# Gate/up weights of a SwiGLU layer: two of the four block sums made by accumulating loads

## Chip, cores and metric

The kernel runs on one core of a Trainium2 chip. The metric is the device time of one execution in microseconds, as the median of several runs. The core's engines are named as the profile names them: PE (TensorE matmuls, with PEld for its weight loads), DVE (VectorE), ACT (ScalarE), POOL (GpSimd) and SP (SyncE, which issues most transfers). Transfers run on 16 DMA engines.

## What is computed

One encoder layer for 512 tokens of width 2048: a combined projection, sliding-window attention and gated linear attention side by side, an output projection, and a SwiGLU feed-forward block of width 5632, with RMS norms between. The part that matters here is the feed-forward block:

```python
h = rmsnorm(x, ffn_norm_w[l])
x = x + (jax.nn.silu(h @ w_gate[l]) * (h @ w_up[l])) @ w_down[l]
```

`w_gate` and `w_up` are 2048 x 5632, `w_down` is 5632 x 2048, all float32.

## The kernel before

Every float32 operand of a matmul is split into a high part (rounded to the PE's fp32r) and a low part (the remainder), and each product is made of three matmuls: high x high, high x low, low x high. The splits are a copy on ACT (high) and a subtraction on DVE (low).

The order of all instructions is written out by hand in the program: each engine executes its own list in order and waits for others by semaphores. Buffers are kept in lists of free slots. The large buffers ("b" in the profile, 16 slots of 128 partitions x 4 KB, `s4` in the code) are handed out in the order in which they came free; a slot can be handed out in the program's order before its last reader has finished on the chip, and the instruction that fills it then waits.

The gate and up projections are run by the class `Feed`. There are 22 column blocks of 256 for each of the two weights, hence 44 units (gate and up alternate), and each unit has four pieces, 176 in all. A piece is a weight block of 512 rows x 256 columns (512 KB). It is handled as two halves, each a 2 x 2 arrangement of 128 x 128 blocks, and multiplied by Strassen's method in Winograd's form: for each half there are seven products in place of eight, each with three matmuls, so a piece has 42 matmuls of 128 x 128 by 128 x 256. This needs, for each half, the raw blocks 11, 12, 21, 22 (three of them as operands of products) and four sums of blocks:

- Z0 = block 12 + block 11, and Z1 = block 21 + block 11 (one DVE instruction, L1095, in which block 11 is broadcast),
- Z2 = Z0 + block 21 (L1096),
- Z3 = Z2 + block 22 (L1097).

The steps of a piece, with their lines:

- `load` (L1073 to L1082): SP issues one transfer of the whole piece into a slot `r`, in rows of 1 KB. Up to three loaded pieces are held ahead of their split.
- `sums` (L1084 to L1097): takes a second slot `S` and has DVE make the four sums.
- `split` (L1099 to L1116): ACT copies the three raw blocks (128x768) and the four sums (128x1024) to two high slots, L1107; DVE makes two low slots, L1112. Then `r` and `S` are given back, and `load` is called again.
- `products` (L1118 to L1141): the 42 matmuls on PE, lines L1137 to L1139, after which the four slots are given back.

`run` (L1183 to L1201) goes through the pieces. For piece i it calls `load`, then `sums` of piece i+2, then `split` of piece i+1, then `products` of piece i, and then one step of pending work, which is mostly `evac`: at the end of a unit, ACT and DVE take the sums out of PSUM (L1153 to L1162) and `finish` scales them and applies SiLU (gate) or multiplies by the gate and stores 512 KB to DRAM from SP (up, L1178 to L1181). The first loads of the stage are issued in the last job of the output projection (`before_out`, L1029). In the last unit `down_start` begins to load for the down projection; its step for piece 3 has POOL reload 16 tiles of the residual (L1244).

Apart from these reloads and 16 residual loads (L954) and 16 stores (L1011) before the stage, POOL has almost nothing to do.

Of the kernel before, what the change touches and what calls it, by code (L numbers as in the profile page):

```python
# [15 lines left out]
F32 = mybir.dt.float32  # L16
# [3 lines left out]
OP = mybir.AluOpType  # L20
# [3 lines left out]
P = 128  # L24
D = 2048
S = 512
KT = D // P
# [28 lines left out]
def _constants():  # L56
# [7 lines left out]
    masks = np.stack([j[:, None] <= j[None, :], j[:, None] >= j[None, :]]).astype(np.uint32)  # L64
    resets = np.ones((2, S), np.float32)
    resets[0, 0::P] = 0.0
# [45 lines left out]
def put(*slots):  # L112
    for s in slots:
        if s.home is not None:
            s.home.free.append(s.i)


def layer(nc, tc, x, attn_norm_w, w_in, rel_table, gw_f, gb_f, gw_b, gb_b, gla_norm_w, w_out,
# [3 lines left out]
    w_gate, w_up, w_down, out = w_gate[0], w_up[0], w_down[0], out[0]  # L122
    pe, act, dve, pool, sp = nc.tensor, nc.scalar, nc.vector, nc.gpsimd, nc.sync
    mm = pe.matmul

    with tc.manual_schedule(), \
# [6 lines left out]
        s4 = Slots(p4, N4, 1024, "b")  # L133
# [73 lines left out]
        def piece512(w, col, kt):  # L207

            ws = w if isinstance(w, list) else [(w, col)]
            n = 512 // len(ws)  # L210
            segs = []
            for i, (wi, c) in enumerate(ws):
                src = wi[kt * P:(kt + 2) * P, c:c + n].rearrange("(k p) c -> p k c", p=P)
                segs.append((src, lambda t, i=i, n=n: t.rearrange("p (k c) -> p k c", k=2)[:, :, i * n:(i + 1) * n]))
            return segs
# [36 lines left out]
        def job(kind, pieces, kts, acts, evac, rate=0.0, before=None, start=None, limit=None):  # L252

            j = Job()
            j.kind, j.kts, j.acts, j.evac, j.rate, j.before, j.start, j.limit = \
                kind, kts, acts, evac, rate, before, start, limit
            j.first = len(st.halves)
            st.add(pieces)
            j.n = len(st.halves) - j.first
            jobs.append(j)  # L260
            return j
# [347 lines left out]
        def gla_operands():  # L609
# [4 lines left out]
            for d, w in enumerate((gw_f[0], gw_b[0])):  # L614
                pool.memset(G["gw"][d].t, 0.0)
                pool.dma_start(out=G["gw"][d].t[16 * d:16 * d + 16], in_=w)
                pool.dma_start(out=G["res"][d].t, in_=c_resets[d:d + 1].to_broadcast([P, S]))

# [379 lines left out]
        def evac_out(c):  # L998
            def f(banks):
                for t in range(4):  # L1000
                    dve.tensor_tensor(x1[c][t].t, x1[c][t].t, banks[t].t, op=OP.add)
                    put(banks[t])
                if c < 3:
                    load_res(c + 1)
                urgent.append(rest())

            def rest():
                yield
                for t in range(4):
                    squares(c, t, x1[c], ss2)  # L1010
                    pool.dma_start(out=xd[4 * c + t], in_=x1[c][t].t)  # L1011
                if c == 3:
                    dve.tensor_reduce(sum2, ss2.rearrange("p (t c) -> p t c", c=4), op=OP.add,
                                      axis=mybir.AxisListType.X)
                    rstd_of(sum2, 4, rstd2, 1.0 / D, scr)
                fs_ = {}
                for q in (2 * c, 2 * c + 1):
                    fs_[q] = [weighted(x1[c], k, W_FFN) for k in (2 * q, 2 * q + 1)]
                    yield
                put(*x1.pop(c))  # L1020
                if c == 3:
                    rb[2] = rows_of(rstd2)
                    rb[3] = s2.get()
                    act.activation(rb[3].t, rb[2].t, AF.Copy, scale=-1.0)
                for q in (2 * c, 2 * c + 1):
                    yield from pair_operands(q, fs_.pop(q))
            return f
# [12 lines left out]
        def start_out(c):  # L1040
            def f():
                if c == 0:
                    free_h()
                    load_res(0)
            return f
# [4 lines left out]
        for c in range(4):  # L1050
            j = job("B", [piece512(w_out, c * 512, k) for k in range(0, KT, 2)], list(range(KT)),
                    lambda k: mixh[k], evac_out(c), rate=1.0, start=start_out(c), before=before_out(c), limit=3)
# [6 lines left out]
        class Feed:  # L1059
# [4 lines left out]
            def __init__(self):  # L1064
# [4 lines left out]
                self.n = len(self.seq)  # L1069
                self.raw, self.S, self.sets = {}, {}, {}  # L1070
                self.n_load = self.n_sums = 0

            def load(self):  # L1073
                while self.n_load < self.n and len(self.raw) < 3 and s4.free:
                    u, q = self.seq[self.n_load]
                    w, j = self.units[u]
                    k = 4 * q
                    r = s4.get(F32, [P, 2, 4, P])
                    sp.dma_start(out=r.t.rearrange("p a b c -> p (a b c)").rearrange("p (k c) -> p k c", k=4),
                                 in_=w[k * P:(k + 4) * P, j * 256:(j + 1) * 256].rearrange("(k p) c -> p k c", p=P))  # L1080
                    self.raw[self.n_load] = r
                    self.n_load += 1  # L1082

            def sums(self, i):  # L1084


                if i != self.n_sums or i >= self.n:
                    return
                self.n_sums += 1
                if i not in self.raw:  # L1090
                    self.load()
                r = self.raw[i].t
                S = self.S[i] = s4.get(F32, [P, 2, 4, P])
                s_ = S.t
                dve.tensor_tensor(s_[:, :, 0:2], r[:, :, 1:3], r[:, :, 0:1].to_broadcast([P, 2, 2, P]), op=OP.add)  # L1095
                dve.tensor_tensor(s_[:, :, 2], s_[:, :, 0], r[:, :, 2], op=OP.add)  # L1096
                dve.tensor_tensor(s_[:, :, 3], s_[:, :, 2], r[:, :, 3], op=OP.add)  # L1097

            def split(self, i):  # L1099
                if i >= self.n or i in self.sets:  # L1100
                    return
                r = self.raw[i]
                parts = [(r.t[:, :, 1:4], [P, 2, 3, P]), (self.S[i].t, [P, 2, 4, P])]
                his = []
                for src, shape in parts:
                    hi = s4.get(F32R, shape)
                    act.copy(hi.t, src)  # L1107
                    his.append(hi)
                out_ = []
                for (src, shape), hi in zip(parts, his):  # L1110
                    lo = s4.get(F32R, shape)
                    dve.tensor_tensor(lo.t, src, hi.f, op=OP.subtract)  # L1112
                    out_.append((hi, lo))
                self.sets[i] = out_
                put(self.raw.pop(i), self.S.pop(i))
                self.load()  # L1116

            def products(self, i, banks):  # L1118
                st_ = self.sets.pop(i)
                piece = self.seq[i][1]  # L1120
                first, last = piece == 0, piece == self.per - 1
                a, z = slice(0, 256), slice(256, 512)
                A, B, C, E = (b.t for b in banks)
                for p in range(2):
                    q = 2 * piece + p
                    (rh, rl), (sh, sl) = st_
                    R = lambda n: (rh.t[:, p, n], rl.t[:, p, n])
                    Z = lambda n: (sh.t[:, p, n], sl.t[:, p, n])
                    x_ = xs[q]
                    prods = [(A[:, a], R(0), x_["B11"], True), (A[:, z], R(2), x_["B21"], False),  # L1130
                             (B[:, a], Z(2), x_["T2"], True), (C[:, a], Z(1), x_["T1"], True),
                             (C[:, z], Z(0), x_["T3"], False), (E[:, a], Z(3), x_["B22"], True),
                             (E[:, z], R(1), x_["T4"], False)]
                    for o, (wh, wl), (xh, xl), head in prods:
                        head = head and first and p == 0
                        end = last and p == 1
                        mm(o, wh, xh, start=head, stop=False, skip_group_check=True)  # L1137
                        mm(o, wh, xl, start=False, stop=False, skip_group_check=True)  # L1138
                        mm(o, wl, xh, start=False, stop=end, skip_group_check=True)  # L1139
                for hi, lo in st_:  # L1140
                    put(hi, lo)  # L1141
# [132 lines left out]
        for h1 in (18, 36, LAST):  # L1274
            for c in range(4):
                j = job("B", [piece512(w_down, c * 512, k) for k in range(h0, h1, 2)], list(range(h0, h1)),
                        lambda k: gT[k], evac_down(c), rate=1.0, before=before_down(h0, c, h1))
# [94 lines left out]
```

## Time and profile before

| | us |
|---|---|
| median of 3 runs (2254.49 to 2255.01) | 2254.79 |
| the profiled execution | 2253.85 |
| its span, first to last instruction | 2252.1 |
| DVE busy in the span | 1453.0 |
| ACT busy in the span | 900.0 |
| POOL busy in the span | 41.0 |

In the lists of groups, a row has the line, the engine, the operation, the tiles (out<-in, buffer numbers left out), the shape and the count; then the busy time, the mean duration in ns, and the idle time of the engine ahead of these instructions with what ended it. In the list of transfers, a row has the size of one and the median time from issue to landing. In the list of DMA queues, a row has the packets, the megabytes and the time that the packets took as a share of the 16 engines' time.

The span has three parts: up to about 870 us attention and the two projections around it, then the gate and up projections, and from about 1763 us the down projection with the final norm.

### The profile page before, as it was taken

The numbers are of one execution on the slowest core, as the hardware profiler recorded it, in microseconds if no ns is written. First come the engines' busy times: TensorE is split into PE (matmuls) and PEld (weight loads), VectorE is DVE, ScalarE is ACT, GpSimd is POOL, SyncE is SP. The second block draws the span as 40 slices with busy tenths as digits, with TensorE's granted clock in tenths as the row PEclk, the third lists the DMA queues.
The fourth block names the chain that finished last, engine by engine and source line by source line (L and its number), as shares of the span: only waits on it lengthen the run. The fifth ranks groups of instructions, "written<-read, shape, count | busy, mean of one in ns | idle before, by whom it ended". The sixth has DMA issues, their size and how long they took to land.

```text
span 2252.1 us, 33983 instructions
## 1 busy us (share of the span) xinstructions
PE 2231.6 (99%) x13662; PEld 2001.0 (89%) x13662; DVE 1453.0 (65%) x2429; ACT 900.0 (40%) x1505; POOL 41.0 (2%) x80
## 2 busy tenths in 40 slices
PE   8999999999999999999999999999999999999998
PEld 6888887888888888999999999999999888888886
DVE  3366665745454446988888888888888623332356
ACT  5344444443444344434444344443444422322332
POOL 1000000000000100000000000000000100000000
PEclk9999999999999999999999999999999999999999
DMA  5525625232324432333333333333334942343312
GB/s 204 157 71 148 181 81 138 82 122 66 101 68 132 140 122 75 113 122 116 118 123 113 118 118 116 126 116 113 122 114 134 340 153 86 123 166 100 116 38 75
DMA packets 193246, 274.02 MB, mean 122 GB/s; under 512 B 13327, under 2 KB 129087, under 8 KB 193088
## 3 DMA queue, kind: packets, MB, share of 16 engines
q1 hardware_dynamic: 188016, 257.07, 36.3%
q0 software_dynamic: 4752, 14.64, 1.9%
q8 instruction: 107, 1.75, 0.3%
q14 instruction: 51, 0.42, 0.1%
q10 hardware_dynamic: 320, 0.14, 0.0%
HBM read 239.24 MB, written 19.99 MB: 115 GB/s over the span
## 4 chain that ended last, share of the span: by engine, by line
PE 97%; DVE 1%; ACT 1%; DMA 0%; issue 0%; SPq 0%; ACTq 0%
PE ps L1139 13%; PE ps L1138 13%; PE ps L1137 13%; PE ps L295 12%; PE ps L293 12%; PE ps L294 12%; PE ps L285 5%; PE ps L286 5%; PE ps L287 5%; PE ps L514 1%; PE ps L841 1%; PE ps L1325 1%; PE ps L1324 1%; PE ps L1326 1%; PE ps L554 1%; PE ps L553 1%
## 5 line engine op out<-in xcount | busy, mean ns | idle before, releaser
L1139 PE MATMUL ps<-a,b 128*128 128x256 f32 x2464 | 698.1, 283 | 2.9 <-DVE b L1112 2.9
L1137 PE MATMUL ps<-a,b 128*128 128x256 f32 x2464 | 697.8, 283 | 0.0
L1138 PE MATMUL ps<-a,b 128*128 128x256 f32 x2464 | 697.6, 283 | 0.0
L1107 ACT CAST b<-b 128x768 fp32r<-128x768 f32 x352 | 326.9, 942 | 405.7 <-DVE b L1112 254.2
L1139 PEld LDWEIGHTS ps<-a,b 128*128 128x128 f32 x2464 | 473.2, 192 | 3.8 <-DVE b L1112 3.8
L1137 PEld LDWEIGHTS ps<-a,b 128*128 128x128 f32 x2464 | 473.2, 192 | 0.0
L1138 PEld LDWEIGHTS ps<-a,b 128*128 128x128 f32 x2464 | 473.2, 192 | 0.0
L197 DVE TENSOR_TENSOR a<-b,a 128x512 fp32r<-128x512 f32 x420 | 279.3, 688 | 252.3 <-ACT a L196 252.0
L1112 DVE TENSOR_TENSOR b<-b,b 128x768 fp32r<-128x768 f32 x352 | 373.0, 1089 | 100.8 <-PE ps L1138 61.8
L293 PE MATMUL ps<-a,a 128*128 128x512 f32 x976 | 382.9, 392 | 0.0
L294 PE MATMUL ps<-a,a 128*128 128x512 f32 x976 | 380.3, 390 | 0.0
L295 PE MATMUL ps<-a,a 128*128 128x512 f32 x976 | 380.3, 390 | 0.0
L196 ACT CAST a<-b 128x512 fp32r<-128x512 f32 x420 | 248.9, 618 | 263.8 <-PE ps L295 239.6
L295 PEld LDWEIGHTS ps<-a,a 128*128 128x128 f32 x976 | 183.2, 188 | 38.4
L294 PEld LDWEIGHTS ps<-a,a 128*128 128x128 f32 x976 | 183.4, 188 | 37.2
L293 PEld LDWEIGHTS ps<-a,a 128*128 128x128 f32 x976 | 183.3, 188 | 37.1
L285 PE MATMUL ps<-a,a 128*128 128x512 f32 x416 | 168.2, 404 | 0.0
L286 PE MATMUL ps<-a,a 128*128 128x512 f32 x416 | 163.3, 393 | 0.0
L287 PE MATMUL ps<-a,a 128*128 128x512 f32 x416 | 163.2, 392 | 0.0
L1095 DVE TENSOR_TENSOR b<-b 128x512 f32<-128x512 f32 x176 | 120.3, 683 | 4.2 <-DMA b<-in_w_up_dram 4.2
L1247 DVE SCALAR_TENSOR_TENSOR a<-ps,small,a 128x512 f32<-128x512 f32 x64 | 45.5, 751 | 118.6 <-PE ps L295 107.5
L578 ACT CAST b<-ps 128x512 fp32r<-128x512 f32 x64 | 37.6, 587 | 144.7 <-PE ps L514 142.8
(197 smaller groups left out, 2314.2 us busy)
## 6 DMA issues: line engine op xcount, KB each, us to landing
b<-in_w_gate_dram SPq DMA_DIRECT2D x88, 512.0 KB, 3.5
b<-in_w_up_dram SPq DMA_DIRECT2D x88, 512.0 KB, 3.6
b<-in_w_down_dram SPq DMA_DIRECT2D x88, 512.0 KB, 4.8
b<-in_w_in_dram SPq DMA_DIRECT2D x96, 256.0 KB, 4.3
b<-in_w_in_dram SPq DMA_DIRECT2D x48, 512.0 KB, 3.9
b<-in_w_out_dram SPq DMA_DIRECT2D x32, 512.0 KB, 4.3
a<-a SPq DMA_DIRECT2D x96, 128.0 KB, 2.3
gd<-b SPq DMA_DIRECT2D x22, 512.0 KB, 2.7
```

The lines of the kernel that those rows point to most:

```text
L197: dve.tensor_tensor(h[3].t, r, h[2].f, op=OP.subtract)
L285: mm(o, wh.t[:, c], xh.t, start=first, stop=False)
L286: mm(o, wh.t[:, c], xl.t, start=False, stop=False)
L287: mm(o, wl.t[:, c], xh.t, start=False, stop=last)
L293: mm(o, xh.t[:, c], wh.t[:, w], start=first, stop=False)
L294: mm(o, xh.t[:, c], wl.t[:, w], start=False, stop=False)
L295: mm(o, xl.t[:, c], wh.t[:, w], start=False, stop=last)
L1107: act.copy(hi.t, src)
L1112: dve.tensor_tensor(lo.t, src, hi.f, op=OP.subtract)
L1137: mm(o, wh, xh, start=head, stop=False, skip_group_check=True)
L1138: mm(o, wh, xl, start=False, stop=False, skip_group_check=True)
L1139: mm(o, wl, xh, start=False, stop=end, skip_group_check=True)
```

## The change

Two of the four sums of each half, Z0 and Z1, are no longer made by DVE. The slot `S` is now taken when the piece is loaded. SP loads block 12 of both halves into S[0] and block 21 of both halves into S[1]; POOL then issues two transfers that read block 11 of both halves from DRAM and add it to S[0] and to S[1] in place (`accum_op`). Each waits for the SP load of the same part of S. Block 11 itself is no longer kept in `r`: SP loads block 12 into `r` with one transfer, and blocks 21 and 22, which lie side by side in DRAM, with another. DVE makes Z2 and Z3 as before. `S` is laid out by sum and then by half, and `r` holds three blocks a half. `load` now needs two free slots.

```diff
             def load(self):
-                while self.n_load < self.n and len(self.raw) < 3 and s4.free:
+                while self.n_load < self.n and len(self.raw) < 3 and len(s4.free) > 1:
                     u, q = self.seq[self.n_load]
                     w, j = self.units[u]
                     k = 4 * q
-                    r = s4.get(F32, [P, 2, 4, P])
-                    sp.dma_start(out=r.t.rearrange("p a b c -> p (a b c)").rearrange("p (k c) -> p k c", k=4),
-                                 in_=w[k * P:(k + 4) * P, j * 256:(j + 1) * 256].rearrange("(k p) c -> p k c", p=P))
+                    r, S = s4.get(F32, [P, 2, 3, P]), s4.get(F32, [P, 4, 2, P])
+                    row = w.ap[0][0]
+                    blocks = lambda a: bass.AP(tensor=w.tensor, offset=w.offset + k * P * row + j * 256 + a,
+                                               ap=[[row, P], [2 * P * row, 2], [1, P]])
+                    for n, a in enumerate((P, P * row)):
+                        sp.dma_start(out=S.t[:, n], in_=blocks(a))
+                    for n in range(2):
+                        pool.dma_start(out=S.t[:, n], in_=blocks(0), accum_op=OP.add)
+                    sp.dma_start(out=r.t[:, :, 0], in_=blocks(P))
+                    sp.dma_start(out=r.t[:, :, 1:3], in_=w[k * P:(k + 4) * P, j * 256:(j + 1) * 256].rearrange(
+                        "(a b p) c -> p a b c", b=2, p=P)[:, :, 1])
                     self.raw[self.n_load] = r
+                    self.S[self.n_load] = S
                     self.n_load += 1
...
                 r = self.raw[i].t
-                S = self.S[i] = s4.get(F32, [P, 2, 4, P])
-                s_ = S.t
-                dve.tensor_tensor(s_[:, :, 0:2], r[:, :, 1:3], r[:, :, 0:1].to_broadcast([P, 2, 2, P]), op=OP.add)
-                dve.tensor_tensor(s_[:, :, 2], s_[:, :, 0], r[:, :, 2], op=OP.add)
-                dve.tensor_tensor(s_[:, :, 3], s_[:, :, 2], r[:, :, 3], op=OP.add)
+                s_ = self.S[i].t
+                dve.tensor_tensor(s_[:, 2], s_[:, 0], r[:, :, 1], op=OP.add)
+                dve.tensor_tensor(s_[:, 3], s_[:, 2], r[:, :, 2], op=OP.add)
...
                 r = self.raw[i]
-                parts = [(r.t[:, :, 1:4], [P, 2, 3, P]), (self.S[i].t, [P, 2, 4, P])]
+                parts = [(r.t, [P, 2, 3, P]), (self.S[i].t, [P, 4, 2, P])]
...
-                    Z = lambda n: (sh.t[:, p, n], sl.t[:, p, n])
+                    Z = lambda n: (sh.t[:, n, p], sl.t[:, n, p])
```

In the changed kernel the loads stand at L1085 (S), L1087 (accumulating), L1088 and L1089 (r), the two adds at L1104 and L1105, and the splits at L1115 (ACT) and L1120 (DVE).

## Prediction

> **What bounds the kernel now.** I read the page's busy times and chain first, then the stage that the change touches (869.9 to 1763.5 us, lines L1137 to L1139) by stretches, then that stage's DVE groups and its DMA. This is the page, and the stretches with the engines' busy times:
>
> ```profile
> span 2252.1 us, 33983 instructions
> PE 2231.6 (99%) x13662; PEld 2001.0 (89%) x13662; DVE 1453.0 (65%) x2429; ACT 900.0 (40%) x1505; POOL 41.0 (2%) x80
> ...
> PE 97%; DVE 1%; ACT 1%; DMA 0%; issue 0%; SPq 0%; ACTq 0%
> ```
>
> ```profile
> 869.90:920.00 50.10, 47.16 (x388) 46.31 (x387) 41.94 (x72) 27.16 (x43) 1.47 (x3) 1.00 0.34 109
> 920.00:1739.00 819.00, 819.00 (x6827) 819.00 (x6827) 716.41 (x1079) 333.98 (x386) 1.08 (x2) 1.00 0.38 119
> 1739.00:1763.50 24.50, 24.50 (x206) 24.50 (x206) 16.89 (x25) 9.43 (x13) 7.44 (x14) 1.00 0.82 291
> ```
>
> The columns of the stretches are the length, then PE, PEld, DVE, ACT, POOL busy, the granted clock, the DMA share and GB/s. From 920 us on PE never idles and its clock is 1.00; a matmul comes every 819.00/6827 = 0.120 us. A piece (128 x 4 weight blocks, 176 of them, 42 matmuls each) takes 42 x 0.120 = 5.04 us. All that PE could gain in the stage is 50.10 - 47.16 = 2.94 us at its start, while DVE is at 716.41/819 = 87% and off the path. So a piece of this stage has a budget of 5.04 us in every resource, and whatever needs more sets the end.
>
> **What goes away.** The DVE groups of the stage, between 1000 and 1600 us, each shape apart:
>
> ```profile
> L1112 DVE TENSOR_TENSOR b<-b,b 128x1024 fp32r<-128x1024 f32 x119 | 145.4, 1222 | 5.7 <-PE ps L1138 5.3 <-ACT a L1153 0.2
> L1112 DVE TENSOR_TENSOR b<-b,b 128x768 fp32r<-128x768 f32 x119 | 113.7, 956 | 60.3 <-PE ps L1138 39.0 <-PE ps L1139 13.3 <-ACT b L1107 6.0
> L1095 DVE TENSOR_TENSOR b<-b 128x512 f32<-128x512 f32 x120 | 82.0, 683 | 0.0
> L1097 DVE TENSOR_TENSOR b<-b,b 128x256 f32<-128x256 f32 x119 | 50.6, 425 | 4.1
> L1096 DVE TENSOR_TENSOR b<-b,b 128x256 f32<-128x256 f32 x119 | 50.6, 425 | 4.1
> ```
>
> L1095 leaves: 0.683 us a piece, 176 x 0.683 = 120 us of DVE. The two adds of 128x256 and the splits stay, in the same sizes, so ACT and PE have the same work in another layout (cost nothing: PE runs beside both). Since PE waits only in the first 50 us, the 120 us are worth between 0 and 2.94 us; I take 1.5.
>
> **What is added, queue by queue.** A piece's one load of 512 KB becomes four on SP (two of 128 KB for S, one of 128 KB and one of 256 KB for r) and two accumulating ones of 128 KB on POOL. The rows for an issue and a landing, from the list of DMA issues, from the views of L1079, L415 and L1244:
>
> ```profile
> b<-in_w_gate_dram SPq DMA_DIRECT2D x88, 512.0 KB, 3.5
> ...
> a<-a SPq DMA_DIRECT2D x96, 128.0 KB, 2.3
> gd<-b SPq DMA_DIRECT2D x22, 512.0 KB, 2.7
> ...
> masks<-in_c_masks_dram POOLq DMA_DIRECT2D x1, 128.0 KB, 4.7
> ```
>
> ```profile
> L1079 SPq DMA_DIRECT2D b<-in_w_gate_dram x88: 367/367/368, 806.0 to 1717.9; - x88
> ```
>
> ```profile
> L415 POOL DMA_DIRECT2D masks<-in_c_masks_dram x1: 768/768/768, 5.5 to 5.5; - x1
> ```
>
> ```profile
> L1244 POOL DMA_DIRECT2D a<-xd x16: 536/536/543, 1731.8 to 1755.3; - x16
> ...
> DMA to landing us min/median/max: 3.0/7.2/9.0
> ```
>
> SP: 4 x 0.367 = 1.47 us of 5.04, under cover. POOL: the masks load has the very shape of an accumulating one (128 partitions x 2 rows of 512 B) and took 0.768 us, so two are 1.54 us of 5.04, also under cover as a rate; POOL would set the pace only from 2.52 us an issue. Both count in the latency below. At the stage's end the reloads of L1244 stand behind the last accumulating loads on POOL; their tiles are first needed after 18 half-pieces of the down projection, so a few us there cost nothing.
>
> DMA engines: rows shrink from 1 KB to 512 B except in the 256 KB load. Two stretches with different packets, 920 to 1680 us and 1775 to 1800 us, give a packet's price:
>
> ```profile
> q1 hardware_dynamic: 82265, 88.95, 37.2%
> ```
>
> ```profile
> q1 hardware_dynamic: 4138, 9.72, 102.4%
> ```
>
> First: 760 x 16 x 0.372 / 82265 = 55.0 ns for 1081 B on average; second: 25 x 16 x 1.024 / 4138 = 99.0 ns for 2349 B. The straight line through both is 17.5 ns + 34.7 ns per 1000 B, hence 35.3 ns for 512 B (an estimate; by bytes alone it is 27.5, by packets alone 55). Per piece and DMA engine: S and the 128 KB of r are 768 packets, 48 an engine, x 35.3 = 1.69 us; the 256 KB are 16 x 55 = 0.88; an eighth of a gd store (8 packets of 4 KB at 17.5 + 142 = 160 ns) 0.16; six completion packets at 17.5 ns 0.10. Together 2.83 us. The accumulating loads add 32 packets an engine at a price that no row shows. Below, it is a plain packet, 35.3 ns (1.13 us, sum 3.96, 79% of 5.04). An accumulation must read the old sum as well as the weight: two packets' worth, 70.6 ns (2.26 us, sum 5.09, 101%). Above, read, read and write one after the other, three packets, 106 ns (3.39 us, sum 6.22, 123%). I take the middle one, because the extra read is a 512 B stream like the others.
>
> [...]
>
> **The latency of a piece.** DVE executes the adds of piece k ahead of the split of piece k-1, so an S that lands late holds a split that PE wants sooner. The timeline of DVE over two units:
>
> ```profile
> 1214.45 2.11 DVE L1112 TENSOR_TENSOR b<-b,b 128x768 fp32r<-128x768 f32 x2
> ...
> 1219.38 1.23 DVE L1112 TENSOR_TENSOR b<-b,b 128x1024 fp32r<-128x1024 f32 x1 [0.42 <-PE ps L1138]
> ...
> 1221.18 0.68 DVE L1095 TENSOR_TENSOR b<-b 128x512 f32<-128x512 f32 x1
> ...
> 1224.41 2.10 DVE L1112 TENSOR_TENSOR b<-b,b 128x768 fp32r<-128x768 f32 x2 [1.63 <-PE ps L1138]
> ```
>
> In the changed order S of piece k takes a buffer that the split of piece k-3 gives back: 1214.45 + 2.11 = 1216.56. The split of piece k-1 starts at 1224.41, when PE gives back its buffers; with two adds of 0.425 ahead, S must be there at 1223.56: 7.0 us without moving anything. That split ends at 1226.51 and PE wants it a piece after 1224.41, at 1229.4: 2.9 us more, 9.9 in all. Now the chain: first S load 2.3 us to landing (the row of 128 KB); POOL issues 2.3 to 3.07 and 3.07 to 3.84; the second accumulation lands 3.0 (the shortest of L1244) to 4.7 us (masks) after its start, 6.1 to 7.8, and with a second read of 16 packets at 35.3 ns 6.7 to 8.4. That fits below 9.9 with idle engines. With full ones it does not: L1244's median is 7.2 us in the stretch where the DMA share is 0.82, which makes 3.07 + 7.2 + 0.56 = 10.8, 0.9 to 1.0 us too late. Once per gate/up pair there is another order. The first S load behind the gd store takes the stored buffer and waits on SP for the store's landing, with the next piece's four loads behind it on SP:
>
> ```profile
> 1212.84 0.34 SPq L1180 DMA_DIRECT2D gd<-b  x1
> ```
>
> 1212.84 + 2.7 = 1215.5, from which 8.0 us are left to 1223.56 and 10.9 to the point where PE waits, 1.0 more than elsewhere, so the same condition decides.
>
> The other new waits hold little. An accumulating load waits on POOL for its S load; behind it stand only further ones, at the start of the stage the last four stores of L1011 (read back only by L1244, at the stage's end), at its end the reloads. On SP each transfer also waits for the one eight transfers before it, two pieces back instead of eight; that one is over 5 us old by then and lands in 2.3 to 3.5, so it costs nothing unless the engines are full.
>
> **The forecast: slower, DMA engines at the brim.** By rate alone 5.09 - 5.04 = 0.05 us x 176 = +9 us. By latency alone, 1.0 us too late in every second piece (the chain spans two) is 88 x 1.0 = +88 us. Both ends assume the doubled accumulation; I take the middle, +48, less 1.5 from DVE: profiled execution 2253.85 (span 2252.1 and 1.75 around it) + 46.5 = 2300.4. The median of the runs, 2254.79, lies 0.94 above the profiled execution; kept out, since it is far within the bounds. Forecast 2300, its own range 2263 to 2342. 42%.
>
> **Rivals.** All is covered: the accumulation costs a plain packet or little more, the engines stay at about 79% and the chain (6.1 to 7.8 us) under 9.9. For it: 2.9 us of spare beyond the idle time, SP, POOL and DVE all far from 5.04. Against it: needs the old sum to be read for next to nothing. Time: 2253.85 + 0.94 less 0 to 2.94, so 2252 to 2255. 37%.
>
> Accumulation far dearer, engines or POOL alone as the bound: at three packets 6.22 - 5.04 = 1.18 us x 176 = +208, 2462; POOL at 3.1 us an issue would give the same. Nothing in the profile speaks for it but that no accumulating load is in it. It decides from 69 ns a packet or 2.52 us an issue. 19%, spread from 2342 to 2480.
>
> Faster than 2250.3: would need over 4.5 us where PE idles 2.94 in the stage. 2%.
>
> **How the numbers follow.** What a measurement can tell from no change is about 0.2%, 4.5 us. Same is the covered case, 0.37; faster 0.02; slower 0.42 + 0.19 = 0.61. The range 2250 to 2400 takes in the covered case, the forecast's own range and the lower quarter of the dear case: 0.37 + 0.42 + 0.05 = 0.84.
>
> **What would show it.** Right: DMA share in the stage from 0.38 to over 0.9; PE waiting for L1120 or L1115, DVE waiting at L1104 for a DMA; POOL's accumulating issues near 0.8 us, as the masks load; landing of an accumulation well above 5 us. Covered instead: PE idle under 3 us in the stage, DMA share near 0.8 or less, DVE's busy share from 87% to 87 - 0.683/5.04 = 73%. Dear instead: DMA share near 1 or POOL busy throughout, and PE idle in every piece. The forecast is wrong in its cause if PE idles but the DMA share stays under 0.85: then an issue or landing time of POOL alone makes the chain late.

## The result and the profile after

| | before | after |
|---|---|---|
| median of the runs, us | 2254.64 (2253.79 to 2255.01) | 2339.99 (2334.21 to 2348.76) |
| ratio | | 1.0383, 95% 1.037 to 1.0395 |
| profiled execution, us | 2253.85 | 2348.76 |

The change costs 85 us. The page of the changed kernel: its busy times, the chain that ended last, and groups of its feed-forward stage.

```profile
span 2347.0 us, 35793 instructions
PE 2271.4 (97%) x13662; PEld 2030.5 (87%) x13662; DVE 1334.2 (57%) x2253; ACT 888.8 (38%) x1505; POOL 461.5 (20%) x432
...
PE 61%; DMA 24%; DVE 9%; issue 4%; SPq 1%; ACT 1%; POOLq 0%; DVEq 0%; ACTq 0%
...
L1147 PE MATMUL ps<-a,b 128*128 128x256 f32 x2464 | 716.3, 291 | 58.0 <-DVE b L1120 57.6
...
L1104 DVE TENSOR_TENSOR b<-b,b 128x256 f32<-128x256 f32 x176 | 74.4, 423 | 299.7 <-DMA b<-in_w_up_dram 217.0 <-DMA b<-in_w_gate_dram 74.0 <-PE ps L295 8.5
```

The row of the kernel before that stands against L1147:

```profile
L1139 PE MATMUL ps<-a,b 128*128 128x256 f32 x2464 | 698.1, 283 | 2.9 <-DVE b L1112 2.9
```

DVE has lost the 119 us that the change takes off it (1453.0 to 1334.2). PE was the whole chain before, at 97%; now 24% of it are loads and 9% DVE. PE idles 58.0 us at L1147 where it idled 2.94 (L1139), and it waits for the split (L1120); DVE in turn stands 291 us at the first add (L1104) until a load of the gate or up weights has landed. The same stretches of the stage as before:

```profile
869.90:920.00 50.10, 48.60 (x401) 47.78 (x400) 38.96 (x67) 27.69 (x44) 21.38 (x20) 1.00 0.77 169
...
920.00:1760.00 840.00, 790.30 (x6285) 780.92 (x6284) 557.59 (x842) 297.42 (x355) 356.90 (x300) 0.97 0.84 177
```

Before, PE was busy without a break from 920 us on, at a clock of 1.00 and a DMA share of 0.38. Now it idles 49.7 us in these 840, its granted clock averages 0.97, and the DMA engines are at 0.84: busy, but not full. The loads themselves, from the view of POOL's line and from the lists of transfers between 1000 and 1600 us:

```profile
L1087 POOL DMA_DIRECT2D b<-in_w_gate_dram x176: 1172/1182/1727, 829.7 to 1813.3; - x176
```

```profile
b<-in_w_gate_dram POOLq DMA_DIRECT2D x108, 128.0 KB, 4.6
...
b<-in_w_up_dram POOLq DMA_DIRECT2D x106, 128.0 KB, 5.0
gd<-b SPq DMA_DIRECT2D x13, 512.0 KB, 5.2
```

An accumulating issue holds POOL for 1.18 us, its data are there 4.6 to 5.0 us after it, and a gd store lands after 5.2 us where it took 2.7.

**Where PE stalls.** Not in every piece or every second one: the long stalls come about once per gate/up pair (eight pieces, 40.3 us of matmuls). One of them, followed from its beginning through the timelines of SP, POOL, DVE and PE; above them stands what SP waited for between 1020 and 1031 us:

```profile
SPq L1085 <- DMA gd<-b: 6.0, 1, 6.0
```

```profile
1021.44 0.41 SPq L1188 DMA_DIRECT2D gd<-b  x1
1027.95 0.89 SPq L1085 DMA_DIRECT2D b<-in_w_up_dram  x2
...
1030.70 2.39 POOL L1087 DMA_DIRECT2D b<-in_w_up_dram  x2 [5.78 <-DVE b L1120]
...
1036.58 0.42 DVE L1104 TENSOR_TENSOR b<-b,b 128x256 f32<-128x256 f32 x1 [4.48 <-DMA b<-in_w_up_dram]
...
1037.38 2.09 DVE L1120 TENSOR_TENSOR b<-b,b 128x768 fp32r<-128x768 f32 x2
...
1038.39 0.39 PE L1147 MATMUL ps<-a,b 128*128 128x256 f32 x1 [1.96 <-DVE b L1120]
```

SP issues the store and then stands 6.0 us, because the next S goes into the buffer just stored. The two S loads go out at 1027.95, and POOL can start 2.75 us later; the add L1104, which reads S[0] and so needs the first of the two accumulating loads, starts 5.9 us after that, at 1036.58, having waited 4.48. That is 8.6 us after the first S load. Behind the adds stands the split of another piece, the one PE wants: PE stalls 1.96 us. (The releaser that POOL's row names, L1120, had ended well before; what POOL waited for last is the S load.)

**What the stall brings with it.** PE alone in stretches of 2 us; behind the length come its busy time, the granted clock, the DMA share and GB/s:

```profile
1036.00:1038.00 2.00, 0.42 (x4) 1.00 1.30 170
1038.00:1040.00 2.00, 1.51 (x8) 0.79 0.36 79
1040.00:1042.00 2.00, 2.00 (x11) 0.50 0.86 234
1042.00:1044.00 2.00, 2.00 (x17) 0.86 0.53 88
1044.00:1046.00 2.00, 2.00 (x19) 1.00 0.90 147
```

For some 3.4 us after the stall the clock is 0.50 and PE does 11 matmuls in 2 us instead of 17. Summed over all 2 us stretches from 860 to 1860 us, the clock's shortfall is 32 us. So the 94.9 us between the two profiled executions are 55.1 of idling (58.0 less 2.94), 32 of half clock and some 8 that I did not place.

### The profile page after: what moved, and what is told of

It is laid out like the page before. It is cut to its first block, busy times and chain, and to the rows that moved or that the text cites. A ratio compares the mean times of both kernels' runs of the same rounds, so it can differ in the third digit from the quotient of the medians.

```text
span 2347.0 us, 35793 instructions
## 1 busy us (share of the span) xinstructions
PE 2271.4 (97%) x13662; PEld 2030.5 (87%) x13662; DVE 1334.2 (57%) x2253; ACT 888.8 (38%) x1505; POOL 461.5 (20%) x432
## 4 chain that ended last, share of the span: by engine, by line
PE 61%; DMA 24%; DVE 9%; issue 4%; SPq 1%; ACT 1%; POOLq 0%; DVEq 0%; ACTq 0%
DMA b<-in_w_up_dram 13%; PE ps L293 11%; PE ps L294 11%; PE ps L295 11%; DMA b<-in_w_gate_dram 7%; DVE b L1120 6%; PE ps L285 5%; PE ps L286 5%; PE ps L287 5%; DMA gd<-b 3%; PE ps L1147 2%; PE ps L1145 2%; PE ps L1146 2%; DVE b L1104 1%; PE ps L514 1%
## 5 line engine op out<-in xcount | busy, mean ns | idle before, releaser
L1147 PE MATMUL ps<-a,b 128*128 128x256 f32 x2464 | 716.3, 291 | 58.0 <-DVE b L1120 57.6
L1145 PE MATMUL ps<-a,b 128*128 128x256 f32 x2464 | 709.6, 288 | 0.0
L1146 PE MATMUL ps<-a,b 128*128 128x256 f32 x2464 | 708.9, 288 | 0.0
L1147 PEld LDWEIGHTS ps<-a,b 128*128 128x128 f32 x2464 | 485.8, 197 | 69.1 <-DVE b L1120 68.9
L1115 ACT CAST b<-b 128x768 fp32r<-128x768 f32 x352 | 317.3, 939 | 543.9 <-DVE b L1120 298.7
L1145 PEld LDWEIGHTS ps<-a,b 128*128 128x128 f32 x2464 | 485.9, 197 | 0.0
L1146 PEld LDWEIGHTS ps<-a,b 128*128 128x128 f32 x2464 | 485.5, 197 | 0.0
L1120 DVE TENSOR_TENSOR b<-b,b 128x768 fp32r<-128x768 f32 x352 | 369.9, 1086 | 26.1 <-ACT b L1115 17.4
L1087 POOL DMA_DIRECT2D b<-in_w_up_dram x176 | 210.4, 1377 | 315.6 <-DMA b<-in_w_up_dram 162.6
L1087 POOL DMA_DIRECT2D b<-in_w_gate_dram x176 | 210.7, 1351 | 273.7 <-DMA b<-in_w_gate_dram 155.6
L1104 DVE TENSOR_TENSOR b<-b,b 128x256 f32<-128x256 f32 x176 | 74.4, 423 | 299.7 <-DMA b<-in_w_up_dram 217.0
```

Source lines behind the costliest of these rows:

```text
L1087: pool.dma_start(out=S.t[:, n], in_=blocks(0), accum_op=OP.add)
```

## The experiments

All are edits of the changed kernel; the ratios are to the kernel before. "The chain" below is worked out from the timelines of SP and DVE: for each piece whose first add waited for a DMA, from the issue of its first S load to that add, 920 to 1760 us, median.

**Is it the addition, or the new structure?** First the same loads without the add, then without the loads.

```diff
-                        pool.dma_start(out=S.t[:, n], in_=blocks(0), accum_op=OP.add)
+                        pool.dma_start(out=S.t[:, n], in_=blocks(0))
```

> Edit: the two loads on GpSimd's queue are plain loads, without the add, into the same places behind the same waits; S0 and S1 then hold the (1,1) block alone, so the output is another one. Same instructions, waits, buffers and bytes read from the weights. If the addition itself makes the chain late (its issue of 1.18 us against some 0.77, and packets of about 65 ns against 36): issue falls to 0.55 to 0.8 us, landing from 4.6 to 2.5 to 3.5 us, the DMA share from 0.84 to about 0.70, and the time to 2253 to 2270 us. If it is the structure (two loads in a row into the same bytes, buffers taken earlier, four SP issues): 2300 us or more even so. Store theory: 2290 to 2320, since SP's waits for the gd store stay.

```diff
-                    for n in range(2):
-                        pool.dma_start(out=S.t[:, n], in_=blocks(0), accum_op=OP.add)
```

> Edit: the two loads on GpSimd's queue are left out; S0 and S1 are the (1,2) and (2,1) blocks, so the output is another one. What is left of the change is four SP loads of 512 B rows, two adds in place of three and the buffers held from the load on. Latency theory: the chain is one load of 2 to 3.5 us, PE idles under 5 us in the stage, 2252 to 2256 us. Structure or store theory: 2275 us or more. It also gives what a packet of 512 B costs without any accumulation in the stage: 35 to 37 ns by the mixture read so far.

Plain: 2254.25 us, ratio 0.9999 (0.999 to 1.0009). Left out: 2252.2 us, 0.999 (0.998 to 1.0). So 512 B rows, four issues on SP, buffers held from the load on and the waits for the gd store (82.8 us in the plain kernel's stage) cost nothing by themselves; the store theory, which had 2290 to 2320 for the plain loads, failed in that form. The plain kernel's POOL line, its stage, and a landing:

```profile
L1087 POOL DMA_DIRECT2D b<-in_w_gate_dram x176 | 124.8, 712 | 316.9 <-DMA b<-in_w_gate_dram 170.1 <-DVE b L1156 48.7 <-DVE b L1104 29.5
```

```profile
920.00:1760.00 840.00, 840.00 (x7000) 839.81 (x6999) 629.08 (x937) 333.52 (x397) 239.99 (x343) 1.00 0.68 199
```

```profile
b<-in_w_up_dram POOLq DMA_DIRECT2D x120, 128.0 KB, 3.2
```

The accumulation makes an issue 1.18 instead of 0.71 us and a landing some 1.8 us longer (5.0 against 3.2 for the up weights); the chain is 8.5 us with it and 6.9 without.

**Is it the engines' rate, or a late chain?** If the engines could not deliver, neither another order on DVE nor two more buffers would help.

```diff
-                    self.sums(i + 2)
                     self.split(i + 1)
+                    self.sums(i + 2)
```

> Edit: on DVE the split of piece i+1 is issued ahead of the sums of piece i+2, everything else as in the changed kernel. Latency theory (a late accumulating load holds the split behind it): the split no longer stands behind the load, which gets the time of about one piece (some 5 us) more, against a lateness of 1 to 3 us; PE's idle time of 51 us in the stage falls below 10 and the granted clock goes back to 1.00: 2255 to 2275 us. Rate theory (the DMA engines cannot deliver a piece in 5.04 us): the order changes nothing, 2325 to 2345 us. Store theory (SP stands behind the gd store's landing once per gate/up pair, 44 times): the late loads remain late by more than a piece there, 2300 to 2330 us.

```diff
-N2 = 70
-N4 = 16
+N2 = 66
+N4 = 18
```

> Edit: 18 buffers of 4 KB in place of 16, paid with 66 of 2 KB in place of 70; order and transfers unchanged. Up to three pieces are loaded ahead as before, but a load takes buffers given back earlier than the split three pieces before, so that its wait on SP for DVE ends sooner. Buffer theory (the S load starts too late because its buffer is late): most of the 85 us come back, 2255 to 2280 us. Rate theory: 2325 to 2345 us. If the chain is late by its own length and SP's order: 2300 to 2340 us. The fewer small buffers may cost something in the stages ahead; the feed-forward stage is read by itself (from 869.9 us on in the changed kernel).

Split first: 2263.27 us, 1.0038 (1.0023 to 1.0053). Two more buffers: 2252.92 us, 0.9994 (0.9984 to 1.0003). All the accumulating loads run in both. The kernel with 18 buffers: its stage, its queues and transfers between 1000 and 1600 us, and what SP waited for in the stage:

```profile
920.00:1760.00 840.00, 840.00 (x7002) 840.00 (x7001) 624.92 (x935) 339.84 (x396) 399.75 (x344) 1.00 0.93 199
```

```profile
q1 hardware_dynamic: 131623, 85.88, 49.3%
q0 software_dynamic: 64722, 31.20, 42.9%
...
b<-in_w_up_dram POOLq DMA_DIRECT2D x120, 128.0 KB, 4.8
```

```profile
SPq L1085 <- PE ps L1146: 243.3, 80, 3.4
SPq L1085 <- PE ps L1147: 223.2, 83, 3.4
```

The engines are at 0.93, an accumulation still lands after 4.8 us, the chain is still 8.5 us, and PE never idles. In the changed kernel SP waited 408.5 us for DVE's L1120, the split that gives the buffer back, and 97.8 for the gd store; with two buffers more it waits for matmuls of a piece further back, and the same chain starts early enough. The rate theory is out: 0.84 in the changed kernel was not a limit but what a stalling PE asks for.

**Why once per pair?** When a pair is done, its two buffers go back, and the very next load takes them, the stored one for S. Two edits let S have the other one. The second also gives S, in the pieces whose buffers come from the split three pieces before, the one that this split returns first:

```diff
-                    put(self.gate)
                     sp.dma_start(out=gd[j], in_=c)
-                    put(c_)
+                    put(c_, self.gate)
```

> Edit: when a gate/up pair is done, its two 4 KB buffers go back in the other order, the stored one first. The load that follows then puts the raw blocks into the stored buffer and S into the other, so that on SP the two S loads go out ahead of the wait for the gd store's landing instead of behind it. Nothing else changes. In the changed kernel PE stalls by 2 us or more about once per pair, each time with some 3.4 us at half clock behind it. Store theory (that wait is what makes S late once per pair): the long stalls go, 2253 to 2275 us, granted clock 1.00. Loop theory (split, load, adds, split of two pieces on takes some 11.2 us against 10.08 whatever the store does, and the lateness adds up over a pair): 2315 to 2345 us.

```diff
-                    r, S = s4.get(F32, [P, 2, 3, P]), s4.get(F32, [P, 4, 2, P])
+                    S, r = s4.get(F32, [P, 4, 2, P]), s4.get(F32, [P, 2, 3, P])
```

> Edit: a load takes its buffer for S ahead of the one for the raw blocks. S then gets the older of the two: in the piece after the gd store that is the buffer that was not stored, and in the others the one that the split three pieces before gives back first, some 1.1 us earlier (one L1120 of 0.95 to 1.2 us). Store theory: as the swap alone, 2253 to 2275 us. Loop theory: a loop of 11.2 us becomes about 10.1, at the brim of 10.08, so 2255 to 2285 us here although the swap alone gives little. Neither expects over 2300 us.

Swapped: 2285.35 us, 1.014 (1.0111 to 1.017), between the two theories. S first: 2253.02 us, 0.9996 (0.9986 to 1.0005). With the swap, the stage, and SP's waits in it, behind those of the changed kernel (the number behind the total is the count):

```profile
920.00:1760.00 840.00, 821.46 (x6702) 809.95 (x6702) 593.69 (x895) 317.01 (x379) 379.42 (x318) 1.00 0.89 188
```

```profile
SPq L1085 <- DVE b L1120: 408.5, 111, 8.0
SPq L1085 <- DMA gd<-b: 97.8, 19, 6.8
```

```profile
SPq L1085 <- DVE b L1120: 396.4, 119, 7.3
SPq L1088 <- DMA gd<-b: 77.1, 20, 5.8
```

The wait for the store has moved from the S loads (L1085) to the raw ones (L1088), and 55 of the 85 us are back. PE still idles 18.5 us of these 840, and SP still waits as long for L1120. Taking S's buffer first gives back the rest; PE's idle time there is 1.5 us. Below it, what the S loads of this kernel wait for in the stage:

```profile
L1147 PE MATMUL ps<-a,b 128*128 128x256 f32 x2464 | 697.7, 283 | 1.5 <-DVE b L1120 1.5
```

```profile
SPq L1085 <- DVE b L1120: 150.6, 42, 4.8
SPq L1085 <- PE ps L1147: 118.5, 71, 3.1
```

This line does more than its expectation says. In the changed kernel S already had the buffer that the split returns first in 73 of the 111 waits for L1120 (by SP's and DVE's timelines), so the 1.1 us could be won only in the other 38. With S first, 42 loads wait for a split, in two of a pair's eight pieces instead of six; 71 wait for matmuls, because their buffer comes back from `products`, as with 18 buffers.

So both are at work: a loop through the split that is a little too long, and one long wait per pair on top of it. The split-first order had 9 us left; with the swap beside it:

> Edit: the order on DVE of e1 (split of i+1 ahead of the sums of i+2) together with the swapped buffers. With that order 9 us over before are left, and SP still waited 115 us for gd stores in the stage. Store theory: the 9 us are these waits, 2252 to 2256 us. If they come from something else (one-time at the stage's start, or ACT's order): 2260 to 2265 us, as with the order alone.

It measured 2252.63 us, 0.9994 (0.9984 to 1.0003): those 9 us were the store waits.

**Lateness by itself, with plain loads.** If only lateness counts, plain loads made late must bring the loss back. Memsets that nobody reads, between the two plain loads (4, then 12, then 8 of them; `idle` is a buffer of 128x160 values made for them):

```diff
-                        pool.dma_start(out=S.t[:, n], in_=blocks(0), accum_op=OP.add)
+                        for _ in range(4 * n):
+                            pool.memset(idle, 0.0)
+                        pool.dma_start(out=S.t[:, n], in_=blocks(0))
```

> Edit: as with plain loads on GpSimd's queue (without the add, output differs in the same way), and between the two loads four memsets of 128x160 values that nobody reads, about 0.95 us on GpSimd in all, which is what the two accumulating issues take more than plain ones (2 x 1.19 against 2 x 0.71). The second load then starts as late as the accumulating one, its packets stay plain ones. If the longer issue on GpSimd alone made the chain late: 2290 us or more. If the longer landing of an accumulating load (4.6 to 5.0 us against 2.8 to 3.2) is needed too: 2253 to 2275 us.

> Edit: as with four memsets between the two plain loads, but with twelve: 12 x 0.237 = 2.84 us. GpSimd then needs 2 x 0.71 + 2.84 = 4.26 us a piece, below the 5.04 of TensorE. Accumulating, the chain is later than plain by 2 x 0.48 of issue, some 1.8 of landing (4.8 against 2.8 to 3.3) and 0.6 to 0.9 of the S load's landing, 3.3 to 3.7 in all; here it is later by 2.84 with plain packets, engines at about 0.67. Lateness theory: what counts is when S is there, whatever made it late; the first 0.95 us cost 2 us of time, 2.84 cost most of the changed kernel's 85: 2290 to 2345 us, with stalls about once per pair and half clock behind them. If the accumulation acts in another way as well (packets that hold up the engines for the other loads, the store's landing): under 2275 us.

> Edit: as with twelve memsets between the two plain loads, but with eight. With twelve, GpSimd went round in 5.1 us (1046.20 to 1051.32), more than TensorE's 5.04, so it was a bound itself and the run told nothing of lateness. Twelve took 3.43 us and 0.28 behind them; eight then make the second load 2.6 us later, at 4.0 us of GpSimd a piece. Lateness theory: four (1.4 us later) cost 2 us of time; 2.6 us lie between that and the accumulating chain's 3.3 to 3.7 and its 85 us: 2262 to 2320 us. If lateness on GpSimd does not count below its own pace: 2253 to 2259 us.

Four: 2256.4 us, 1.0012 (1.0002 to 1.0021). Eight: 2256.9 us, 1.0011 (1.0002 to 1.0021), below what the lateness theory had given. Twelve: 2278.91 us, 1.0113 (1.0098 to 1.0129), between its two expectations, but that run shows something else too, as POOL's timeline tells:

```profile
1041.10 1.41 POOL L1090 DMA_DIRECT2D b<-in_w_gate_dram  x2 [0.28 <-issue]
1042.50 3.43 POOL L1089 MEMSET idle<- 128x160 f32 x12
1046.20 0.71 POOL L1090 DMA_DIRECT2D b<-in_w_gate_dram  x1 [0.28 <-issue]
...
1051.32 1.41 POOL L1090 DMA_DIRECT2D b<-in_w_up_dram  x2 [0.28 <-issue]
```

POOL goes round in 5.1 us here without waiting for a load, against 5.04 of PE: it has become a bound itself, so the run can't be read for lateness alone. And the runs with four and eight had put the delay in the wrong place. Who waits for POOL's loads, in the run with eight:

```profile
who waited for it (us, times):
  DVE b L1107: 170.0, 82
  ACT b L1118: 25.4, 17
```

L1107 is the first add, and it reads S[0]: it waits for the first of the two loads only. S[1] is read by the split (L1118 on ACT) a step later, where there was room for the 1.4 or 2.6 us. So a delay between the two is not in the chain, which measured 7.1 us in both. (The expectation of the last run, on record before I saw this, still gives another reason, that the second load lands sooner when it starts later; that was a misreading, and no load there landed in under 2.5 us.) The last run puts the delay behind the S load's landing and ahead of both loads, where it is in the chain either way:

```diff
+                    for _ in range(5):
+                        pool.memset(S.t[:, 0], 0.0)
                     for n in range(2):
-                        pool.dma_start(out=S.t[:, n], in_=blocks(0), accum_op=OP.add)
+                        pool.dma_start(out=S.t[:, n], in_=blocks(0))
```

> Edit: plain loads on GpSimd's queue again (no add, output differs), and ahead of the first of them five memsets of 128x256 values of S's first block, which the plain load then overwrites. They must wait for the S load's landing, so that they lengthen the chain where nothing else shortens it; some 1.6 us in all by the 128x160 form's 0.237, GpSimd some 3.0 us a piece. Delays between the two loads did not lengthen it: from the first S load's issue to an add that waited for a DMA, the median is 6.9 us plain, 7.1 with four and 7.1 with eight memsets between, 8.5 in the changed kernel (the second load landed sooner when it started later). Here it should come to about 8.5 with plain packets and the engines at 0.65 or less. Lateness theory: 2310 to 2350 us, PE stalling 1.5 to 3 us about once per pair, half clock behind it. If the accumulation's packets must be there too: under 2275 us.

It measured 2313.21 us, 1.0268 (1.0249 to 1.0286), with a chain of 7.75 us, shorter than the 8.5 aimed at. Its stage, and one of its stalls:

```profile
920.00:1760.00 840.00, 810.27 (x6565) 799.31 (x6564) 579.64 (x875) 309.56 (x370) 462.88 (x1091) 0.99 0.63 184
```

```profile
1637.37 0.58 PE L1149 MATMUL ps<-a,b 128*128 128x256 f32 x1 [2.21 <-DVE b L1122]
```

No accumulation, engines at 0.63, and PE stalls by 2 us as in the changed kernel. Put together, by the chain's length:

| kernel | chain, us | time, us |
|---|---|---|
| plain | 6.9 | 2254.25 |
| plain, 4 memsets between | 7.1 | 2256.4 |
| plain, 8 between | 7.1 | 2256.9 |
| plain, 12 between (POOL a bound itself) | 7.65 | 2278.91 |
| plain, 5 ahead | 7.75 | 2313.21 |
| accumulating (the changed kernel) | 8.5 | 2339.99 |
| accumulating, swapped | 8.1 | 2285.35 |
| accumulating, 18 buffers | 8.5 | 2252.92 |
| accumulating, S's buffer first | 9.7 | 2253.02 |

With order and buffers as in the change, the time breaks away between 7.1 and 7.75 us, whether or not anything is added; with 18 buffers or S's buffer first, a chain of 8.5 or 9.7 us costs nothing.

**Both repairs together.** The split-first order and S's buffer first, all sums still made by the loads:

> Edit: both repairs that cost no memory together: on DVE the split of i+1 ahead of the sums of i+2, and S's buffer taken ahead of the raw one. All sums still made by the loads as in the change. Before the change PE idled 2.94 us in the stage; no ordering can win more than that. Lateness theory: 2250 to 2254 us, at or up to 3 us under the kernel before. If the loads' extra traffic costs anything that is not lateness: 2256 us or more.

It measured 2252.0 us, ratio 0.999 (0.9982 to 0.9999): 2.2 us below the kernel before, at the edge of what these runs can tell apart.

```profile
L1147 PE MATMUL ps<-a,b 128*128 128x256 f32 x2464 | 698.2, 283 | 1.0 <-DVE b L1120 1.0
```

PE's idle time went from 2.94 to 1.0 us, which is about what was won.

## Why the prediction was right, and where not

The direction and the range held, the 2300 was 40 us short, and its cause was half wrong. That the range held is in part luck: 2340 lies 2 us inside its upper end, and the 85 us came about in another way than the 88 us which set that end.

- **DVE's 120 us, taken as worth 1.5 (0 to 2.94).** Right: with the loads left out the kernel is 2.1 us faster, and with everything repaired 2.2.
- **POOL's issue, 0.768 us from the masks row.** Mis-sized: that is a plain load's price (0.71 in the run without the add); accumulating it is 1.18. As a rate it stays under cover, 2.4 of 5.04 us. In the chain it stands once and not twice, as the prediction had it, because the first add needs only the first of the two loads; the two errors about cancel. That POOL would be a bound from 2.52 us an issue is borne out by the twelve memsets: a round of 5.1 us, and the time went up.
- **The packet price, 70.6 ns.** The number was nearly right: the 18-buffer run gives 0.429 x 16 x 600 us / (239 loads x 256 rows) = 67.3 ns (239 from its list: 120 up and 119 gate loads), against 36.0 for the packets of SP's queue (0.493 x 16 x 600 / 131623). The working behind it was not: it doubled a plain row of 35.3 ns, but without the add the same rows on the same queue take 0.179 x 16 x 600 / (238 x 256) = 28.2 ns (in a kernel whose engines are less full), so an accumulating row cost 2.4 plain ones here. That the old sum is read as a second packet was an estimate of mine; the runs show the price of a row, not what it is made of. SP's queue was costed too high: its 1024 weight packets a piece were to average 40 ns. So the sum is not 5.09 but 0.93 x 5.04 = 4.7 us.
- **"DMA engines at the brim", +9 by rate.** This step failed. At 0.93 PE does not idle at all, so the rate term is zero. The prediction had named the sign of it: PE idle with a share under 0.85 means that issue and landing alone make the chain late. The share was 0.84.
- **The latency: 7.0 us without moving anything, 9.9 until PE waits; a chain of 6.7 to 8.4 "fits below 9.9 with idle engines".** This step failed, and it is the one that matters. The chain was 8.5 us, just above that range, and 8.5 is below 9.9; yet it cost 85 us. The 2.9 us between the bounds are a reserve that is spent once. In six of a pair's eight pieces (the 111 waits for L1120), by the order in which buffers come back, there is a loop: the split of piece k-3 returns S's buffer, the chain follows, then the adds of k, and behind them on DVE the split of k-1; two pieces on, the same again. Two pieces are 10.08 us; 2.09 for the split and 0.80 from first add to split leave 7.2 for the chain, close to the 7.0 that the prediction had; where S takes the buffer that the split returns first, 1.1 more. In the timeline of SP, two such turns in a row take 20.3 us from the S load of a pair's second piece to that of its sixth, and 21.7 us from the third to the seventh (medians), where 20.16 are to be had; with the swap, where the clock stays up almost throughout, 21.0 and 21.1, in the plain kernel 19.7 and 20.2. So the loop loses up to 0.8 us a turn, and then comes the eighth piece, whose S stands behind the gd store. There PE pays: 44 of the 49 us that it idles between 920 and 1760 us stand before the seventh piece of a pair, whose split is held on DVE by the late add of the eighth. The runs show the bound (nothing lost at 6.9, little at 7.1, much at 7.75); that the loop is the reason follows from these turns and from the repairs, each of which opens it in another place, and was not tried in a further way.
- **The store order once per pair: "the same condition decides".** Failed. It was worked out with 2.7 us for the store's landing and weighed against the 9.9. The store took 5.2, the wait put S later by several us (6.0 in the example), and moving that wait behind the S loads alone gave back 55 of 85 us.
- **The latency term, 88 pieces by 1.0 us = +88.** Near the measured 85, and still not a hit: the stalls are fewer, about one per pair and mostly 1.4 to 3.4 us long, and a third of the loss is no wait at all but the clock behind it, which the prediction didn't have.
- **The rivals.** "All is covered" was one buffer order away: S first gives it, at 2253. The dear accumulation (106 ns) is out at 67.3.

## What to carry to other kernels

A change that moves work from an engine to the loads has to be checked as a loop, not as a rate: go from the instruction that returns the buffer through the loads to the next return, and compare that with as many pieces as the loop spans. Which instruction returned the buffer has to be read from the queue's waits for every piece of the pattern; here they were not the same. Slack that shows up as "the consumer wants it only later" is spent once and must not be added to the allowance of every turn. If the loop is too long, the order in which buffers are taken and the order on the engine that consumes them are cheaper to change than the transfers: here one swapped line took back all 85 us, and with both repairs the change is worth about 2 us, most of what PE had idled before.

## What the hardware showed that I had not expected

- **PE ran at half clock behind many of its stalls.** In the changed kernel every stall of 1.9 us or more was followed by 3.4 us at 0.50 (the longest, 4.90 us, by 6.8). Between 1.3 and 1.8 us it went either way: in the changed kernel one of 1.36 us left the clock alone, in the swapped one 1.34 us did not. With five memsets ahead, stalls of 1.93, 2.12 and 2.27 us left it alone, so the length alone does not decide.

```profile
1398.94 0.39 PE L1147 MATMUL ps<-a,b 128*128 128x256 f32 x1 [1.36 <-DVE b L1120]
```

```profile
1400.00:1402.00 2.00, 1.92 (x16) 1.00 0.73 189
```

```profile
1532.71 0.39 PE L1147 MATMUL ps<-a,b 128*128 128x256 f32 x1 [1.34 <-DVE b L1120]
```

```profile
1530.00:1532.00 2.00, 1.37 (x12) 1.00 0.63 160
1532.00:1534.00 2.00, 1.13 (x7) 1.00 1.30 256
1534.00:1536.00 2.00, 2.00 (x11) 0.55 0.92 231
```

The first two rows are the changed kernel's, the others the swapped one's. In the split-first kernel, where PE idled 3.08 us in all between 920 and 1760 us, the clock stayed at 1.00:

```profile
920.00:1760.00 840.00, 836.92 (x6939) 833.47 (x6939) 622.90 (x928) 332.69 (x391) 395.75 (x335) 1.00 0.92 195
```

What went with half clock can be worked out from the clock records of the changed kernel's trace and PE's idle times between 880 and 1850 us. All half-clock stretches begin on one grid with a step of 3.413 us, and each lasts one step, the last of them (from 1844.7 us) two. The 18 steps in which PE idled 1.70 us or more in all were each followed by half clock; of those with 1.62 us or less only one was, with 1.34 us, and it was at half clock already. With five memsets ahead the matmuls at half clock (0.41 in place of 0.28 us) give a grid with the same step. There a stall of 1.57 us inside one step left the clock alone and one of 1.76 us inside one step did not; those of 1.93, 2.12 and 2.27 us lie across two steps, with no more than some 1.4 us in one. The swapped kernel got there with less: PE idled 1.50 us in all from 1530 to 1534 us (0.63 and 0.87 by the rows above), and 0.55 followed. So in the changed kernel, and for these stalls with five memsets ahead, the idle time within one step, and not the length of the stall, tells which stalls were followed by half clock; the swapped kernel's line lies lower, and why is not shown.

- **An accumulating load was dearer to issue and slower to land, not only on the engines.** 1.18 against 0.71 us on POOL and 4.6 to 5.0 against 2.8 to 3.2 us to landing, beside 67.3 against 28.2 ns a row on the engines. The packets differ too: in the plain kernel, between 1000 and 1600 us, this queue moves its 31 MB in 11450 packets (the row below); with the add it takes 64722 (the 18-buffer kernel's row, further up).

```profile
q0 software_dynamic: 11450, 31.31, 17.9%
```
